# Short feed-forward: gate operands in steps between down-projection tiles, up-projection over 512 columns

## Chip, cores and metric

The kernel runs on one core of one Trainium2 chip. The metric is the device time of one execution in microseconds; a lower time is better.

## What is computed

A transformer layer is applied to two sequences with the same weights, a long one of 1024 tokens and a short one of 512, each with 16 learned tokens ahead. Everything is float32. Cut to what matters:

```python
n = rms_norm(h); qa, ka, va, qb, kb, vb = split(n @ w_in)
h = h + concat(gqa(qa, ka, va), diff_attention(qb, kb, vb)) @ w_out
n = rms_norm(h)
gate = n @ w_ff_gate                                   # 1024 -> 2816
gate = conv3_over_positions(gate) + conv_b             # depthwise, width 3
h = h + (gelu(gate) * (n @ w_ff_up)) @ w_ff_down       # 2816 -> 1024
y = rms_norm(h)[:, 16:]
```

## The kernel before

Activations lie transposed: features on the 128 partitions, tokens along the free dimension. The width of 1024 is 8 tiles (`KT`), the feed-forward width of 2816 is 22 tiles of 128 (`NFF`).

Float32 products are made of three matmuls. `split` (L111) turns an operand into a rounded part `hi` (a cast on ScalarE, ACT in the profile, L114) and the rest `lo` (a subtraction on VectorE or GpSimd, L115). `mm3` (L118) then issues hi x hi, hi x lo and lo x hi (L121 to L123). `dense` (L126) does that for the 8 tiles of the contraction: 24 matmuls into one PSUM tile.

`load_weight` (L171) fetches a 512 KB weight tile into a buffer `w_f` (2 of them) and splits it into `w_hi` and `w_lo` (3 of each in the short feed-forward). All loads and most stores are issued by SyncE (SP in the profile), whose queue is in order.

Order of the work: the short sequence's projection comes first, then its attention beside the long projection. Then the short sequence's output projection and feed-forward (`mixer_out`, `conv_glu`) run beside the long sequence's attention. Both are Python generators that yield their cost; `merge` (L1234) draws from them in the ratio of 1 to 0.4. That gives the program order. A scheduler that simulates a time line then sets each engine's order: among the instructions that it holds to be ready, the earlier in the program goes first. On the chip each engine keeps to the order so found. The rest, the long sequence's output projection and feed-forward, follows alone.

The short feed-forward, `conv_glu` with s = 1, N = 512, goes over the 22 tiles in groups of two (`grp`, f0 = 0, 2, ... 20):

1. Gate: per tile two chunks of 258 columns (256 and the neighbours that the convolution needs) through `dense`; the convolution on ScalarE and VectorE (L784 to L787) writes the tile `gate`, of which there is one buffer. One GELU over the group (L790).
2. Up: per tile the chunks of `centres = even_chunks(N, 510)`, two of 256 columns, through `dense`; VectorE multiplies the PSUM tile into `gate` (L802), and `split` makes `a_hi` (ScalarE) and `a_lo` (GpSimd) of it (L803).
3. Down: two weight tiles `wd`; 8 output tiles of 512 columns (`down`, L808), each of 2 x 3 matmuls, added to `h` by VectorE (L814).

PSUM has two banks for all of these ("mm").

The long feed-forward needs sums and differences of quarters of its first two gate weight tiles, split into hi and lo. `presplit` (L868) makes them ahead of time, in the short feed-forward's group f0 = 12 (`FPRE`): it loads the two raw weight tiles into the two `w_f` buffers, forms four sums of 512 columns on VectorE in a tile of the tag `gate` (L886, `minus` L881), and four times (`kept`, L874) splits a tile and stores both parts in DRAM (`wg`). Its order is `kept(0)`, the first raw tile as it is; two sums and `kept(1)`; two sums and `kept(2)`; `kept(3)`, half of the second raw tile. In the program all of it stands between the up- and the down-projection of that group, with two yields of cost 0. Since the two `wd` tiles hold two of the three `w_hi` buffers until the down-projection has ended, the splits share the third.

Of the kernel before, what the change touches and what calls it, by code (L numbers as in the profile page):

```python
# [15 lines left out]
ALU = mybir.AluOpType  # L16
# [36 lines left out]
def even_chunks(total, cap):  # L53
    cnt = -(-total // cap)
    w = -(-total // cnt)
    w += w % 2
    out, c = [], 0
    while c < total:
        out.append((c, min(w, total - c)))
        c += w  # L60
    return out
# [32 lines left out]
def pool(ctx, g, name, bufs, side):  # L94
    return ctx.enter_context(g.tc.tile_pool(name=name, bufs=bufs, side=side, reuse_waits="tile"))
# [15 lines left out]
def split(g, hi, lo, src, lo_engine=None):  # L111

    nc = g.nc
    return (nc.scalar.copy(hi, src).ins,  # L114
            (lo_engine or nc.vector).tensor_tensor(out=lo, in0=src, in1=hi.bitcast(F32), op=ALU.subtract).ins)  # L115
# [10 lines left out]
def dense(g, ps, w, xhi, xlo, c0, cw, order=range(KT)):  # L126

    for i, k in enumerate(order):
        last = mm3(g, ps, *block(w, k), xhi[k][:, c0:c0 + cw], xlo[k][:, c0:c0 + cw], i == 0, i == KT - 1)
    return last  # L130
# [17 lines left out]
def load_whole(wp, g, src, tag="w_f"):  # L148
    w = wp.tile([P, D], F32, name=tag, tag=tag, bufs=2)
    g.nc.sync.dma_start(out=w, in_=src)  # L150
    return w
# [19 lines left out]
def load_weight(g, wp, src, bufs=2, ahead=2, lo_engine=None):  # L171

    nc = g.nc
    w = wp.tile([P, D], F32, name="w_f", tag="w_f", bufs=ahead)
    nc.sync.dma_start(out=w, in_=src)
    hi = wp.tile([P, D], F32R, name="w_hi", tag="w_hi", bufs=bufs)
    lo = wp.tile([P, D], F32R, name="w_lo", tag="w_lo", bufs=bufs)
    passes = split(g, hi, lo, w, lo_engine)
    if g.splits is not None:
        g.splits.append(passes)  # L180
    return hi, lo
# [566 lines left out]
def conv_glu(ctx, g, s, st, side, wp, wb, gb):  # L748

    nc, tc = g.nc, g.tc  # L750
    N = SEQS[s]
# [5 lines left out]
    with tc.tile_pool(name=f"fn{s}", bufs=2, side=side, reuse_waits="tile") as np_:  # L757
        for c0, cw in token_chunks(s):
            for k in range(KT):
                t = np_.tile([P, cw], F32, name="t", tag="t")  # L760
                nc.vector.scalar_tensor_tensor(out=t, in0=h[:, k, c0:c0 + cw],
                                               scalar=g.gain[:, V_GFFN + k:V_GFFN + k + 1],
                                               in1=rstd[:, c0:c0 + cw], op0=ALU.mult, op1=ALU.mult)
# [3 lines left out]
    ap = pool(ctx, g, f"fa{s}", 2, side)  # L767
    centres = even_chunks(N, 510)
    for f0 in range(0, NFF, G):
# [5 lines left out]
        for f, c0, cw in ([(f, *c) for c in centres for f in grp] if f0 == 0 and s == 0 else  # L775
# [7 lines left out]
            a = gate[:, f - f0, c0:c0 + cw]  # L783
# [10 lines left out]
        for f in grp:  # L794
            wu = load_weight(g, wp, g.w_up[f], bufs=wb)
            ahi = ap.tile([P, N], F32R, name="a_hi", tag="a_hi", bufs=G + 1 - s)
            alo = ap.tile([P, N], F32R, name="a_lo", tag="a_lo", bufs=G + 1 - s)
            for c0, cw in centres:
                up = g.psum.tile(P, cw, "mm")
                dense(g, up, wu, xhi, xlo, c0 + 1, cw)  # L800
                a = gate[:, f - f0, c0:c0 + cw]
                nc.vector.tensor_tensor(out=a, in0=up, in1=a, op=ALU.mult)  # L802
                split(g, ahi[:, c0:c0 + cw], alo[:, c0:c0 + cw], a, nc.gpsimd)  # L803
                yield 24 * cw
            acts.append((ahi, alo))
        wd = [load_weight(g, wp, g.w_down[f], bufs=wb) for f in grp]

        def down(j, c0, cw):  # L808
            ps = g.psum.tile(P, cw, "mm")
            for i, ((ahi, alo), (dhi, dlo)) in enumerate(zip(acts, wd)):  # L810
                mm3(g, ps, dhi[:, j * P:(j + 1) * P], dlo[:, j * P:(j + 1) * P],
                    ahi[:, c0:c0 + cw], alo[:, c0:c0 + cw], i == 0, i == len(acts) - 1)
            hs = h[:, j, 1 + c0:1 + c0 + cw]
            nc.vector.tensor_tensor(out=hs, in0=ps, in1=hs, op=ALU.add)  # L814

        if f0 == FPRE:
            yield from presplit(g, wp, ap)
        if grp[-1] < NFF - 1:
            for j in range(KT):
                for c0, cw in even_chunks(N, 512):  # L820
                    down(j, c0, cw)
                    yield 3 * len(grp) * cw
            continue
        op = pool(ctx, g, f"fo{s}", 2, side)
        ob = 2 - s
        cw = 256
# [41 lines left out]
def presplit(g, wp, ap):  # L868

    nc = g.nc  # L870
    raw = [load_whole(wp, g, g.w_gate[i]) for i in range(2)]
    a11, a12, a21, a22 = (w[:, i * H:(i + 1) * H] for w in raw for i in range(2))

    def kept(i, src, w=D):  # L874
        hi = wp.tile([P, D], F32R, name="w_hi", tag="w_hi", bufs=3)[:, :w]
        lo = wp.tile([P, D], F32R, name="w_lo", tag="w_lo", bufs=3)[:, :w]
        split(g, hi, lo, src)
        for part, tl in enumerate((hi, lo)):
            nc.sync.dma_start(out=g.wg[i, part, :, :w], in_=tl.bitcast(F32))

    def minus(out, a, b):  # L881
        nc.vector.tensor_tensor(out=out, in0=a, in1=b, op=ALU.subtract)

    kept(0, raw[0])
    t = ap.tile([P, 2, H], F32, name="gate", tag="gate", bufs=1)
    nc.vector.tensor_tensor(out=t[:, 0], in0=a21, in1=a22, op=ALU.add)  # L886
    minus(t[:, 1], t[:, 0], a11)
    kept(1, t.rearrange("p x c -> p (x c)"))
    yield 0

    minus(t[:, 1], a12, t[:, 1])
    minus(t[:, 0], a11, a21)
    kept(2, t.rearrange("p x c -> p (x c)"))
    kept(3, a22, H)
    yield 0


def winograd(g, wp, up, x, raw, c0, cw, pre=None):
# [348 lines left out]
def drain(gen):  # L1247
    for _ in gen:
        pass
# [4 lines left out]
FPRE = 12  # L1254
# [16 lines left out]
def trunk_kernel(ctx, tc, g):  # L1271
# [82 lines left out]
    def sample():  # L1354
        yield from mixer_out(g, 1, st1, "left", wp, 3, "mm")
        yield from conv_glu(es1, g, 1, st1, "left", wp, 3, 1)
# [85 lines left out]
```

## Time and profile before

| | |
|---|---|
| median of 3 runs | 2126.57 us (2126.3 to 2130.99) |
| profiled execution | 2138.1 us, span 2136.3 us |
| mean granted TensorE clock | 0.982 |
| busy: TensorE matmul, weight load | 2051.1 us (96%), 1833.1 us (86%) |
| busy: VectorE, ScalarE, GpSimd | 1724.1 us (81%), 1156.8 us (54%), 582.7 us (27%) |
| HBM over the span | 138 GB/s |

PE is TensorE's matmuls, PEld its weight loads, DVE VectorE, ACT ScalarE, POOL GpSimd, and SPq the queue of SyncE. A row of the time line gives the start and the duration in us, the engine, the line, the operation, what it writes and reads, the shape and a count; in brackets the idle time of the engine ahead of it and what ended it. Matmuls are pipelined, so a matmul's duration overlaps the next one's. The profiled execution is 11.5 us longer than the median of the timed runs.

### The profile page before, as it was taken

To read this page: it belongs to the slowest core of one execution; us is meant where nothing else is said; L and a number is where in the kernel's file an instruction comes from. 1 tells how busy PE (TensorE), PEld (TensorE's weight loads), DVE (VectorE), ACT (ScalarE), POOL (GpSimd) and SP (SyncE) were. 2 spreads that over 40 slices of the span, in tenths; PEclk is the share of its full clock that TensorE was granted. 3 is DMA by queue.
4 is the path that set the end of the run, shared out by engine and by line. 5 is a ranking of instruction groups with operands and counts; after the bars stand their busy time and mean duration, and the time that the engine had idled before them with its cause. 6 is when DMAs were issued, how large, how long until landed. Compare 5 with 4: busy or idle time off the path is not lost.

```text
span 2136.3 us, 35264 instructions
## 1 busy us (share of the span) xinstructions
PE 2051.1 (96%) x12302; PEld 1833.1 (86%) x12302; DVE 1724.1 (81%) x3786; ACT 1156.8 (54%) x2253; POOL 582.7 (27%) x534
## 2 busy tenths in 40 slices
PE   6999999999999999999999999979999999999998
PEld 6988888997887999899989999978888777778877
DVE  6878889767879788888988885578878878869886
ACT  6635566544657556666666765345444444435454
POOL 4653233553112000000000000542444444330112
PEclk8999999999999999999999999998999999999999
DMA  7564335456621322223352224986232232247443
GB/s 252 178 198 133 118 110 170 153 182 226 206 84 55 105 75 70 70 85 114 103 188 77 93 88 145 300 256 229 101 109 89 97 115 84 94 166 258 119 126 126
DMA packets 164897, 296.30 MB, mean 139 GB/s; under 512 B 21456, under 2 KB 82672, under 8 KB 164208
## 3 DMA queue, kind: packets, MB, share of 16 engines
q1 hardware_dynamic: 162416, 287.76, 41.6%
q0 software_dynamic: 2304, 6.29, 0.8%
q8 instruction: 97, 1.59, 0.3%
q14 instruction: 80, 0.66, 0.1%
HBM read 211.13 MB, written 82.85 MB: 138 GB/s over the span
## 4 chain that ended last, share of the span: by engine, by line
PE 76%; DVE 12%; DMA 4%; ACT 3%; issue 3%; POOL 1%; SPq 1%; DVEq 0%; ACTq 0%; POOLq 0%
PE ps_mm L121 17%; PE ps_mm L123 17%; PE ps_mm L122 17%; PE ps_t L456 5%; PE ps_s L431 3%; PE ps_s L432 3%; PE ps_s L121 2%; PE ps_s L122 2%; PE ps_s L123 2%; PE ps_o L471 2%; PE ps_o L470 2%; DVE p L433 1%; DVE w_lo L115 1%; DMA m<-oT 1%; DVE acc L979 1%
## 5 line engine op out<-in xcount | busy, mean ns | idle before, releaser
L121 PE MATMUL ps_mm<-xhi,w_hi 128*128 128x258 f32 (+3 forms) x1264 | 383.4, 304 | 12.0 <-ACT xhi L114 3.7
L122 PE MATMUL ps_mm<-xlo,w_hi 128*128 128x258 f32 (+3 forms) x1264 | 379.0, 300 | 0.3 <-POOL xlo L115 0.3
L123 PE MATMUL ps_mm<-xhi,w_lo 128*128 128x258 f32 (+3 forms) x1264 | 377.2, 299 | 0.3 <-DVE w_lo L115 0.3
L433 DVE TENSOR_SCALAR_CACHE_REDUCE p<-ps_s 114x344 f32<-114x344 f32 (+4 forms) x562 | 257.6, 488 | 30.2 <-PE ps_s L432 19.1
L114 ACT CAST pt_hi<-ps_t 128x512 fp32r<-128x512 f32 (+6 forms) x360 | 169.3, 483 | 181.0 <-PE ps_t L456 155.2
L121 PEld LDWEIGHTS ps_mm<-xhi,w_hi 128*128 128x128 f32 x1264 | 240.0, 190 | 17.5 <-ACT xhi L114 5.4
L438 ACT ACTIVATE p<-p,nm 114x1040 f32<-114x1040 f32 (+5 forms) x212 | 214.8, 1013 | 72.8 <-DVE nm L436 71.8
L115 DVE TENSOR_TENSOR w_lo<-w_f,w_hi 128x1024 fp32r<-128x1024 f32 (+1 forms) x182 | 192.8, 1067 | 66.2 <-ACT w_hi L114 65.6
L122 PEld LDWEIGHTS ps_mm<-xlo,w_hi 128*128 128x128 f32 x1264 | 240.3, 190 | 1.9 <-POOL xlo L115 0.7
L123 PEld LDWEIGHTS ps_mm<-xhi,w_lo 128*128 128x128 f32 x1264 | 240.0, 190 | 1.2 <-DVE w_lo L115 0.5
L114 ACT CAST w_hi<-w_f 128x1024 fp32r<-128x1024 f32 (+1 forms) x199 | 167.6, 856 | 84.9 <-PE ps_mm L122 57.5
L115 DVE TENSOR_TENSOR pt_lo<-ps_t,pt_hi 128x512 fp32r<-128x512 f32 (+4 forms) x312 | 171.7, 561 | 43.7 <-ACT pt_hi L114 42.3
L115 POOL TENSOR_TENSOR a_lo<-gate,a_hi 128x256 fp32r<-128x256 f32 x44 | 43.3, 985 | 545.3 <-ACT a_hi L114 525.9
L431 PE MATMUL ps_s<-k,q 128*114 128x348 f32 (+4 forms) x552 | 183.6, 338 | 3.4 <-DVE p L433 3.2
L456 PE MATMUL ps_t<-ident,p 128*128 128x128 f32 (+7 forms) x1188 | 183.0, 270 | 1.0 <-DVE nm L436 0.5
L432 PE MATMUL ps_s<-k,q 128*114 128x348 f32 (+4 forms) x552 | 171.1, 315 | 0.0
L121 PE MATMUL ps_s<-xhi,w_hi 128*128 128x256 f32 (+4 forms) x480 | 148.7, 313 | 20.4 <-ACT xhi L234 8.2
L456 PEld LDWEIGHTS ps_t<-ident,p 128*128 128x128 f32 (+7 forms) x1188 | 140.4, 136 | 29.6 <-issue 6.8
L123 PE MATMUL ps_s<-xhi,w_lo 128*128 128x256 f32 (+4 forms) x480 | 147.4, 307 | 1.4 <-DMA w_lo<-wo 1.4
L122 PE MATMUL ps_s<-xlo,w_hi 128*128 128x256 f32 (+4 forms) x480 | 148.6, 310 | 0.0
L121 PE MATMUL ps_mm<-t_hi,w_hi 128*128 128x512 f32 (+2 forms) x368 | 144.6, 393 | 1.2 <-DVE v L934 1.2
L123 PE MATMUL ps_mm<-t_hi,w_lo 128*128 128x512 f32 (+2 forms) x368 | 144.4, 392 | 0.1
(275 smaller groups left out, 5309.4 us busy)
## 6 DMA issues: line engine op xcount, KB each, us to landing
w_f<-w_gate SPq DMA_DIRECT2D x46, 512.0 KB, 3.5
w_f<-w_up SPq DMA_DIRECT2D x44, 512.0 KB, 3.4
w_f<-w_in SPq DMA_DIRECT2D x36, 512.0 KB, 3.9
a_f<-act SPq DMA_DIRECT2D x62, 256.0 KB, 2.7
w_f<-w_down SPq DMA_DIRECT2D x22, 512.0 KB, 3.3
act<-a_t SPq DMA_DIRECT2D x44, 256.0 KB, 2.1
a<-w_down SPq DMA_DIRECT2D x40, 256.0 KB, 5.4
w_hi<-wo SPq DMA_DIRECT2D x36, 256.0 KB, 5.1
```

The costliest lines, as they stand in the source:

```text
L114: return (nc.scalar.copy(hi, src).ins, (lo_engine or nc.vector).tensor_tensor(out=lo, in0=src, in1=hi.bitcast(F32), op=ALU.subtract).ins)
L115: (lo_engine or nc.vector).tensor_tensor(out=lo, in0=src, in1=hi.bitcast(F32), op=ALU.subtract).ins)
L121: nc.tensor.matmul(ps, lhsT=whi, rhs=xhi, start=start, stop=False)
L122: nc.tensor.matmul(ps, lhsT=whi, rhs=xlo, start=False, stop=False)
L123: return nc.tensor.matmul(ps, lhsT=wlo, rhs=xhi, start=False, stop=stop).ins
L431: nc.tensor.matmul(ps, lhsT=q[0], rhs=k[:, c0:c0 + cw], start=True, stop=False)
L432: nc.tensor.matmul(ps, lhsT=q[1], rhs=k[:, c0:c0 + cw], start=False, stop=True)
L433: nc.vector.tensor_scalar(out=p[:, c0:c0 + cw], in0=ps, scalar1=HD ** -0.5, scalar2=-3.0e38, op0=ALU.mult, op1=ALU.max, accum_out=mx[:, i: ...
L438: g.last_exp = nc.scalar.activation(p, p, AF.Exp, bias=nm, accum_out=l).ins
L456: nc.tensor.transpose(tps[:, c:c + M], p[:, k0:k0 + kw], g.ident[:M, :M])
L470: nc.tensor.matmul(o, lhsT=v[:, i, :], rhs=hi, start=i == 0, stop=False)
L471: nc.tensor.matmul(o, lhsT=v[:, i, :], rhs=lo, start=False, stop=False)
```

## The change

1. The up-projection's chunks are `even_chunks(N, 512)`: one of 512 columns for the short sequence. Everything that runs by chunk (24 matmuls, the product L802, the split L803, the yield) runs once per tile over 512 columns.
2. `presplit` is no longer drawn as a whole ahead of the down-projection. One step of it is drawn after each of the group's 8 down-projection tiles (there are six steps, ended by five yields); what is left is drained behind them.
3. Its order of steps is: loads, two sums; `kept(1)`; two sums; `kept(2)`; `kept(0)`; `kept(3)`.
4. The four sums are made on GpSimd instead of VectorE.

```diff
-            for c0, cw in centres:
+            for c0, cw in even_chunks(N, 512):
                 up = g.psum.tile(P, cw, "mm")
                 dense(g, up, wu, xhi, xlo, c0 + 1, cw)
...
-        if f0 == FPRE:
-            yield from presplit(g, wp, ap)
         if grp[-1] < NFF - 1:
+            pre = presplit(g, wp, ap) if f0 == FPRE else iter(())
             for j in range(KT):
                 for c0, cw in even_chunks(N, 512):
                     down(j, c0, cw)
                     yield 3 * len(grp) * cw
+                next(pre, None)
+            drain(pre)
             continue
...
     def minus(out, a, b):
-        nc.vector.tensor_tensor(out=out, in0=a, in1=b, op=ALU.subtract)
-
-    kept(0, raw[0])
+        nc.gpsimd.tensor_tensor(out=out, in0=a, in1=b, op=ALU.subtract)
+
     t = ap.tile([P, 2, H], F32, name="gate", tag="gate", bufs=1)
-    nc.vector.tensor_tensor(out=t[:, 0], in0=a21, in1=a22, op=ALU.add)
+    nc.gpsimd.tensor_tensor(out=t[:, 0], in0=a21, in1=a22, op=ALU.add)
     minus(t[:, 1], t[:, 0], a11)
+    yield
     kept(1, t.rearrange("p x c -> p (x c)"))
-    yield 0
+    yield
 
     minus(t[:, 1], a12, t[:, 1])
     minus(t[:, 0], a11, a21)
+    yield
     kept(2, t.rearrange("p x c -> p (x c)"))
+    yield
+    kept(0, raw[0])
+    yield
     kept(3, a22, H)
-    yield 0
```

## The prediction

> **What bounds the kernel now.** I read the page's busy times first, then the busy time by stretches, then the instructions in order of time where a stretch falls short.
>
> ```profile
> span 2136.3 us, 35264 instructions
> ...
> PE 2051.1 (96%) x12302; PEld 1833.1 (86%) x12302; DVE 1724.1 (81%) x3786; ACT 1156.8 (54%) x2253; POOL 582.7 (27%) x534
> ```
>
> TensorE is busy nearly throughout. The changed code runs from about 690 to 1345 us, beside the attention of the long sequence. Columns of the stretches: length, then busy time of PE, PEld, DVE, ACT and POOL, then the granted TensorE clock, the DMA share and GB/s.
>
> ```profile
> 640.00:1060.00 420.00, 416.99 (x2819) 379.53 (x2820) 361.18 (x987) 264.00 (x465) 37.16 (x46) 1.00 0.27 84
> ...
> 1101.00:1123.00 22.00, 18.41 (x114) 16.90 (x113) 17.93 (x49) 13.73 (x26) 0.00 (x0) 0.84 0.52 176
> ```
>
> For 420 us TensorE has work at full clock: there only fewer or shorter matmuls save time, and DVE, ACT or POOL savings are worth nothing by themselves. The exception is 1101 to 1123 us, right behind the gate pair that the change moves (f0 = 12). There PE idles 3.6 us and the clock falls:
>
> ```profile
> 1090.00:1101.00 11.00, 10.53 (x57) 8.92 (x56) 11.00 (x25) 5.61 (x11) 0.00 (x0) 1.00 0.58 223
> ...
> 1112.80:1116.20 3.40, 0.31 (x4) 0.10 (x2) 3.05 (x8) 3.40 (x9) 0.00 (x0) 0.91 0.39 118
> 1116.20:1122.30 6.10, 6.10 (x24) 5.57 (x25) 4.20 (x12) 5.24 (x11) 0.00 (x0) 0.50 0.38 138
> ```
> ```profile
> 1112.82 0.28 PE L123 MATMUL ps_mm<-xhi,w_lo 128*128 128x258 f32 x1
> 1116.19 1.51 PE L545 MATMUL ps_o<-o_sq,ones_v 128*128 128x342 f32 x2 [3.09 <-ACT o_sq L543]
> ```
>
> I call this the hole. Its price: 3.1 us idle, 6.10 x (1 - 0.50) = 3.05 us lost at half clock, so 6.2 us. No other stretch of this stage offers as much.
>
> **Part 1: up-projection in one chunk of 512.** It replaces 22 x 2 x 24 = 1056 matmuls of 256 columns by 528 of 512. Matmuls overlap, so I price them by start to start: 14 steps between the first pair of rows (all rows between are of that kind), 9 between the second.
>
> ```profile
> 693.92 0.29 PE L121 MATMUL ps_mm<-xhi,w_hi 128*128 128x256 f32 x1
> ...
> 695.58 0.28 PE L123 MATMUL ps_mm<-xhi,w_lo 128*128 128x256 f32 x1
> ...
> 710.75 0.40 PE L121 MATMUL ps_mm<-a_hi,w_hi 128*128 128x512 f32 x1
> ...
> 712.85 0.40 PE L470 MATMUL ps_o<-pt_hi,v 128*128 128x512 f32 x1
> ```
>
> 1.66 / 14 = 118.6 ns and 2.10 / 9 = 233.3 ns. Two small ones cost 237.2, one large 233.3: 3.9 ns x 528 = 2.0 us saved, all on the path. The durations in the rows (0.28 against 0.40) would promise 0.16 x 528 = 84 us, but they include the overlap. The 528 weight loads that vanish ran beside matmuls already: nothing.
>
> The eviction is halved in number and grows in size, first the rows of now, then the nearest rows of 512 columns:
>
> ```profile
> L802 DVE TENSOR_TENSOR gate<-ps_mm,gate x44: 399/419/425, 690.2 to 1341.0; 128x256 f32<-128x256 f32 x44
> L114 ACT CAST a_hi<-gate x44: 388/406/420, 691.5 to 1341.8; 128x256 fp32r<-128x256 f32 x44
> L115 POOL TENSOR_TENSOR a_lo<-gate,a_hi x44: 728/766/1702, 691.9 to 1342.9; 128x256 fp32r<-128x256 f32 x44
> ```
> ```profile
> L114 ACT CAST w_hi<-a_f 128x512 fp32r<-128x512 f32 x62 | 38.5, 622 | 24.5 <-PE ps_mm L123 11.9 <-DMA a_f<-act 11.4 <-PE ps_mm L122 0.9
> ...
> L1024 DVE TENSOR_TENSOR act<-ps_mm,act 128x512 f32<-128x512 f32 x44 | 29.9, 679 | 0.8 <-ACT act L1016 0.8
> L1032 POOL TENSOR_TENSOR a_t<-act 128x512 f32<-128x512 f32 x22 | 28.8, 1310 | 27.3 <-DMA act<-act 22.4 <-DVE act L1024 4.9
> ```
>
> DVE: 44 x 0.419 - 22 x 0.679 = 3.5 us less; ACT: 44 x 0.406 - 22 x 0.622 = 4.2 us less; both beside a full TensorE, so zero. But the last chunk's way to the down-projection lengthens by 0.26 + 0.22 + 0.54 = 1.0 us, eleven times. What covers it now:
>
> ```profile
> 1079.48 0.28 PE L123 MATMUL ps_mm<-xhi,w_lo 128*128 128x256 f32 x1
> ...
> 1083.81 0.39 PE L122 MATMUL ps_mm<-a_lo,w_hi 128*128 128x512 f32 x1
> ```
> ```profile
> 1082.26 0.74 POOL L115 TENSOR_TENSOR a_lo<-gate,a_hi 128x256 fp32r<-128x256 f32 x1 [4.49 <-ACT a_hi L114]
> ```
>
> The last up matmul starts at 1079.48, its a_lo is ready at 1083.00 and first used at 1083.81; attention and the first operand's matmuls fill the time between. Of the 1.0 us, 0.8 is slack and 0.2 would be seen if the order stayed: eleven times 2 us; at most 11 us if no slack existed elsewhere; below nothing it cannot go by itself. The order of instructions is planned anew and TensorE has attention to put there, so I take 0. Sum of part 1: -2.0 us, bounds -2.0 and +9.
>
> **Part 2: the pair step by step, sums on GpSimd.** The work is the same: two weight loads, four sums of 512 columns, four splits, eight stores, in another place. Four DVE sums go (first and last shown; 0.68, 0.68, 0.68, 0.67 = 2.7 us):
>
> ```profile
> 1083.70 0.68 DVE L886 TENSOR_TENSOR gate<-w_f 128x512 f32<-128x512 f32 x1
> ...
> 1094.06 0.67 DVE L882 TENSOR_TENSOR gate<-w_f 128x512 f32<-128x512 f32 x1
> ...
> 1101.58 0.68 DVE L115 TENSOR_TENSOR w_lo<-w_f,w_hi 128x512 fp32r<-128x512 f32 x1
> ...
> 1104.09 1.21 DVE L115 TENSOR_TENSOR w_lo<-w_f,w_hi 128x1024 fp32r<-128x1024 f32 x1
> ```
>
> GpSimd gets 4 x 1.31 = 5.2 us (the a_t row); its queue is otherwise empty here, so nobody queues behind them. Whether the 2.7 us are worth anything depends on the chain that makes the hole:
>
> ```profile
> 1079.68 1.05 ACT L114 CAST w_hi<-w_f 128x1024 fp32r<-128x1024 f32 x1 [0.71 <-PE ps_mm L122]
> ...
> 1099.71 0.62 ACT L114 CAST w_hi<-w_f 128x512 fp32r<-128x512 f32 x1 [0.15 <-DMA wg<-w_hi]
> ...
> 1100.69 1.05 ACT L114 CAST w_hi<-w_f 128x1024 fp32r<-128x1024 f32 x1
> ...
> 1112.07 1.05 ACT L114 CAST w_hi<-w_f 128x1024 fp32r<-128x1024 f32 x1 [3.02 <-DMA w_f<-w_up]
> ```
> ```profile
> 1094.75 0.33 SPq L175 DMA_DIRECT2D w_f<-w_gate  x1
> ...
> 1102.65 0.42 SPq L175 DMA_DIRECT2D w_f<-w_gate  x1
> ...
> 1105.95 3.31 SPq L175 DMA_DIRECT2D w_f<-w_up  x2
> ```
> ```profile
> w_f<-w_gate SPq DMA_DIRECT2D x46, 512.0 KB, 3.5
> ```
>
> Read backwards: TensorE waits for o_sq on ACT; ACT had stood 3.02 us before a weight cast whose load (w_up[14]) had not landed, with the eviction of the gate product and o_sq queued behind it. That load was issued at 1105.95, right after its w_f buffer came free: the buffer's DVE split began at 1104.09 and took 1.21, though its cast was done at 1101.74. So DVE cost 2.35 us there. It also carried the pair's last split (1101.58), whose end at 1102.26 freed the other buffer for the load at 1102.65. A DVE that has done 2.7 us less by then can issue the load up to 2.35 us earlier, and the 3.02 us stand would shrink to 0.7.
>
> Against this stand two things. First, GpSimd sums slow DVE. This GpSimd instruction and the DVE one beside it, then the same DVE instruction without company:
>
> ```profile
> 700.62 0.73 POOL L115 TENSOR_TENSOR a_lo<-gate,a_hi 128x256 fp32r<-128x256 f32 x1 [3.37 <-ACT a_hi L114]
> ```
> ```profile
> 700.69 1.23 DVE L508 TENSOR_SCALAR p<-p,r 128x1040 f32<-128x1040 f32 x1
> ...
> 703.05 0.76 DVE L508 TENSOR_SCALAR p<-p,r 128x1040 f32<-128x1040 f32 x1
> ```
>
> 0.47 us are lost beside 0.73 us of GpSimd; four sums of that loss take back 1.9 of the 2.7, four of twice the length 3.8. The Trainium skill has a rule for it ("SBUF — State Buffer", Who interferes with whom): the shared port pair is an exclusive lock, and whoever comes second waits for the whole instruction. By that rule four sums could hold DVE for their full 5.2 us, more than it saves, and the hole would stay: the sum would be part 1 alone. The trace agrees that DVE waits (0.47 of the 0.66 us in which the two overlap).
>
> Second, the order. `kept(0)` moves from first to third of four splits, `kept(3)` stays last, and these two release the two w_f buffers that the next group's gate loads wait for. The splits now start every (1099.71 - 1079.68) / 3 = 6.7 us, since two of the three w_hi buffers are held by the down-projection and each split must be stored before the next. If `kept(0)` still runs first whenever its buffer is free and the sums aren't done, nothing is late. If it waits its turn, the first split starts when the two GpSimd sums end, at 1083.00 + 2 x 1.31 = 1085.6 plus waits, and the last one 6 us later than now. The eight stores and two loads also change places on SP; a store that waits for its split holds up the q loads behind it. Attention has q buffers in hand, so I put that at zero, at most one split's 6.7 us.
>
> I take half of the hole for part 2: 3.1 us gained, because the DVE relief is about half eaten by GpSimd. Bounds: 6.2 gained, 9.8 lost (rival C).
>
> **Sum.** -2.0 - 3.1 = -5.1 us. The profiled execution took 2138.1 us (span 2136.3), 11.5 over the median 2126.57, so a part of what it shows may not be in the timed runs; the hole depends on when a load lands, which is one more reason for half. On the median: 2126.6 - 5.1 = 2121.5.
>
> **Rivals.** A: the hole closes, -2.0 - 6.2 = 2118.4. For it: in 420 us of the same loop without the pair PE misses 3 us, so the pair alone makes the hole, and its own chain (2.35 us of DVE wait) is nearly as long as ACT's stand. It also closes with less than that if the half clock needs the whole idle: in the 420 us, with only short waits, the clock stays at 1.00, and 0.50 follows the one idle of 3.1 us. Then half of the idle removed takes all of the slow part with it: 1.5 + 3.05 + 2.0 = 6.6 us, 2120.0; of A's chance 0.07 is this. The Trainium skill states such a rule ("TensorE: Matmul & The Clock Gate", The two states you'll see): the array falls to half rate after an idle window of about 3.4 us. By it the sum is that 2120.0, and the trace agrees as far as its one idle goes.
>
> B: the hole stays, because DVE's relief is used up or the load is late for SP's sake: -2.0, 2124.6. For it: DVE is busy 11.00 of 11 us from 1090 to 1101, so what is taken off may be filled by attention at once, and the loads land when the DMA queues allow.
>
> C, slower: `kept(0)` and `kept(3)` hold the two w_f buffers longer. The next gate weights then come 6 to 7 us late, while FF has nothing else to give TensorE; a second idle of 6.7 with another 3.05 of half clock on top of a hole that stays: -2.0 + 9.8 = +7.8, 2134.4. It decides from 8.4 us of new waiting. For it: program order now puts `kept(0)` after the sums, and the load at 1102.65 follows its buffer's release at once. Against it: `kept(0)` needs no sum and finds the buffer free at 1079.68; the cast at 1100.69 came 2.4 us or so after its load could have landed (issue 1094.75, 3.5 us from issue to landing by the last row above), so the first weights have some slack.
>
> That the 512 chunk changes nothing is within the forecast: it is worth 2.0 us at most.
>
> **How the numbers follow.** Chances: forecast (part of the hole goes) 0.38, A 0.29, B 0.19, C 0.14. A measurement of this kernel tells 0.3%, 6.4 us, from no change: the line lies at 2120.2 and 2132.9. Faster: A, plus the part of the forecast that ends under 2120.2 (0.10) = 0.39. Slower: C less its mild half, plus waits of part 1, 0.13. Same: 0.48. The range reaches from A with 3 us to spare, 2115.5, to most of C, 2132; between them lie 0.82. The likeliest case's own range is 2119 to 2124.
>
> **What would show it.** Up matmuls of 512 columns with starts 0.233 us apart; four GpSimd sums around 1083 to 1095 us and no DVE sum of 512 columns there; the wait of the next group's weight cast for its w_up load under 1.5 us, and the granted clock near 1.00 in the 22 us behind the pair's down-projection. I am wrong if the stage behind it shows a longer wait of a cast for w_gate (C), if down matmuls wait for a_lo more than 2 us in all, or if the new order opens holes elsewhere in the stage, which no row of before can show.

## The result and the profile after

The change costs time: 2140.27 us median (2134.69 to 2145.5, five runs) against 2126.57 us. The ratio on record is 1.0052 (95% interval 1.0038 to 1.0067); these two medians alone give 1.0064. The forecast was 2121.5 us, in a range from 2115.5 to 2132.

The profiled execution of after was its shortest (2134.69), that of before (2138.1) longer than any of its timed runs; side by side these two would show a gain. So both kernels were profiled again, with the experiments: "before again" (span 2128.1) and "after again" (span 2139.1). Their difference, 11.0 us, is nearly that of their medians (2130.5 and 2141.06), and they are compared below.

First the two stretches of after that answer to the prediction's (columns as there). The stretch in which the hole stood is full and at full clock. But the gate pair now runs some 28 us earlier (its four GpSimd sums start from 1055.17 to 1064.48 us), so this stretch no longer lies right behind it; what became of the hole is read below, over 1050 to 1130 us.

```profile
640.00:1060.00 420.00, 415.77 (x2490) 362.23 (x2488) 349.92 (x919) 256.78 (x432) 34.30 (x34) 1.00 0.26 83
...
1101.00:1123.00 22.00, 22.00 (x126) 19.47 (x125) 19.25 (x50) 16.69 (x29) 1.40 (x1) 1.00 0.34 107
```

The up-projection's rows in the time line of after start 0.23 us apart, as priced:

```profile
691.60 0.39 PE L121 MATMUL ps_mm<-xhi,w_hi 128*128 128x512 f32 x1
691.83 0.39 PE L122 MATMUL ps_mm<-xlo,w_hi 128*128 128x512 f32 x1
692.06 0.39 PE L123 MATMUL ps_mm<-xhi,w_lo 128*128 128x512 f32 x1
```

The loss lies elsewhere. The next two fences show, for before again and after again, when two kinds of instruction ran: L802, VectorE's product of the up-projection, and L433, VectorE's eviction of the attention scores. After the count come the shortest, median and longest duration in ns, then the first and the last start in us (L433's first belongs to the short sequence).

```profile
L802 DVE TENSOR_TENSOR gate<-ps_mm,gate x44: 398/419/425, 686.9 to 1335.6; 128x256 f32<-128x256 f32 x44
L433 DVE TENSOR_SCALAR_CACHE_REDUCE p<-ps_s x562: 401/508/522, 162.5 to 1257.5; 114x344 f32<-114x344 f32 x72, 128x344 f32<-128x344 f32 x64, 128x264 f32<-128x264 f32 x21, 102x264 f32<-102x264 f32 x16
```
```profile
L802 DVE TENSOR_TENSOR gate<-ps_mm,gate x22: 672/690/692, 689.4 to 1301.5; 128x512 f32<-128x512 f32 x22
L433 DVE TENSOR_SCALAR_CACHE_REDUCE p<-ps_s x562: 401/509/523, 163.1 to 1296.1; 114x344 f32<-114x344 f32 x72, 128x344 f32<-128x344 f32 x64, 128x264 f32<-128x264 f32 x21, 102x264 f32<-102x264 f32 x16
```

Before, the last scores were evicted at 1257.5 us, and the up-projection went on until 1335.6. After, the up-projection ends at 1301.5 and the last scores come only at 1296.1. The short feed-forward has run ahead of the long attention, so that little is left beside the attention's end. What that costs is in the busy times by stretches, before again and then after again:

```profile
1250.00:1300.00 50.00, 49.75 (x356) 46.74 (x355) 34.57 (x69) 28.67 (x55) 4.06 (x4) 1.00 0.40 134
1300.00:1350.00 50.00, 49.78 (x361) 49.30 (x360) 23.60 (x61) 23.20 (x46) 16.15 (x20) 1.00 0.71 210
1350.00:1400.00 50.00, 48.23 (x307) 45.98 (x306) 29.86 (x52) 18.79 (x44) 26.89 (x37) 1.00 0.95 303
```
```profile
1250.00:1300.00 50.00, 50.00 (x317) 45.99 (x316) 41.84 (x112) 31.68 (x58) 1.29 (x1) 1.00 0.25 76
1300.00:1350.00 50.00, 46.63 (x307) 42.43 (x306) 27.31 (x69) 23.82 (x57) 6.65 (x8) 0.97 0.44 124
1350.00:1400.00 50.00, 43.57 (x255) 39.33 (x254) 30.27 (x51) 20.38 (x48) 30.57 (x44) 1.00 0.97 324
```

From 1300 to 1400 us PE was busy 98.0 us, now 90.2, and 1.4 us more go at the lower clock (0.03 of 46.63). The waits of PE in after again from 1294 to 1400 us (total, times, longest) are those of a chain with little beside it: the attention's last normalisations (o_sq, o_rs) and the start of the long output projection (operands xhi, weights wo from DRAM).

```profile
PE ps_s L121 <- ACT xhi L114: 2.5, 2, 1.9
PE ps_s L121 <- DMA w_hi<-wo: 2.1, 4, 1.5
PE ps_s L123 <- DMA w_lo<-wo: 1.5, 3, 0.9
PE ps_o L545 <- ACT o_sq L543: 1.3, 2, 1.1
PE ps_o L466 <- DVE o_rs L106: 0.9, 1, 0.9
```

**A measure for all runs.** "Lost" is worked out from the starts of the matmul rows: each step from one start to the next, less the median step between the same two kinds where PE stands full (before again, 690 to 1000 us; 0.233 us for the 512-column matmuls). It holds idle time and slow clock alike. How finely the kinds are told apart moves the differences between kernels in the first "lost" column by up to 4 us, in the two behind it by about 1. "Cover" is the feed-forward work left behind the attention's last score matmul: its matmul rows times their step, without the last group's down-projection (96 rows of 256 columns, 11.3 us), which lies behind the last score in every kernel but two_evict and before_mm3, where 12 of its rows do. One profiled execution stands for each kernel: up512_only's was its slowest (2.5 us over its median), up512_late's its fastest (3.1 us under). All in us:

| kernel | ratio (95% interval) | cover | lost: first up product to last score | last score to last down-projection | from there to first long gate product | span |
|---|---|---|---|---|---|---|
| before again | 0.9996 (0.9984 to 1.0008) | 45.4 | 27.0 | 4.0 | 19.9 | 2128.1 |
| steps_only | 1.0015 (1.0002 to 1.0027) | 46.2 | 26.7 | 4.3 | 19.8 | 2128.2 |
| steps_dve | 0.9997 (0.9985 to 1.0009) | 45.4 | 24.7 | 4.5 | 19.0 | 2126.9 |
| mid_steps | 1.0015 (1.0004 to 1.0027) | 39.7 | 25.4 | 4.6 | 21.7 | 2133.1 |
| up512_mid | 0.9987 (0.9976 to 0.9998) | 36.7 | 22.0 | 4.0 | 23.0 | 2123.0 |
| up512_late | 1.0001 (0.999 to 1.0013) | 32.0 | 22.0 | 4.3 | 25.2 | 2125.3 |
| one_evict | 1.0007 (0.9996 to 1.0019) | 31.3 | 25.2 | 4.3 | 21.2 | 2130.9 |
| up512_early | 1.0036 (1.0022 to 1.005) | 12.1 | 25.2 | 8.1 | 24.2 | 2137.4 |
| up512_only | 1.0053 (1.0037 to 1.0069) | 7.7 | 24.3 | 13.5 | 26.0 | 2143.9 |
| after again | 1.0045 (1.003 to 1.006) | 5.6 | 27.5 | 12.4 | 21.1 | 2139.1 |
| two_evict | 1.0132 (1.0112 to 1.0152) | 0 | 26.4 | 21.6 | 28.5 | 2152.5 |
| before_mm3 | 1.0166 (1.0148 to 1.0185) | 0 | 42.4 | 19.9 | 30.4 | 2168.6 |
| up512_paced | 1.007 (1.0056 to 1.0085) | 40.6 | 38.1 | 5.0 | 23.6 | 2146.7 |
| after_paced | 1.008 (1.0066 to 1.0094) | 40.9 | 38.0 | 7.1 | 25.4 | 2150.5 |
| after_fine | 1.0132 (1.0115 to 1.0149) | 41.3 | 49.2 | 4.7 | 26.0 | 2158.8 |
| up512_fine | 1.0151 (1.0131 to 1.0171) | 41.1 | 53.2 | 4.6 | 25.5 | 2161.8 |

The measure closes to about 1 us: over the whole span, the 2.0 us of saved steps taken off, it gives after again +9.9 against before again (spans +11.0) and two_evict +24.3 (spans +24.4).

### The profile page after: what moved, and what is told of

Its sections match the earlier page's. It is cut to its first block, busy times and chain, and to the rows that moved or that the text cites. A ratio compares the mean times of both kernels' runs of the same rounds, so it can differ in the third digit from the quotient of the medians.

```text
span 2132.9 us, 34150 instructions
## 1 busy us (share of the span) xinstructions
PE 2047.8 (96%) x11774; PEld 1798.5 (84%) x11774; DVE 1724.4 (81%) x3760; ACT 1153.0 (54%) x2231; POOL 585.2 (27%) x516
## 3 DMA queue, kind: packets, MB, share of 16 engines
q1 hardware_dynamic: 162416, 287.76, 41.3%
## 5 line engine op out<-in xcount | busy, mean ns | idle before, releaser
L121 PE MATMUL ps_mm<-xhi,w_hi 128*128 128x258 f32 (+4 forms) x1088 | 353.4, 325 | 11.3 <-ACT xhi L114 4.2
L122 PE MATMUL ps_mm<-xlo,w_hi 128*128 128x258 f32 (+4 forms) x1088 | 349.2, 321 | 0.4 <-POOL xlo L115 0.3
L123 PE MATMUL ps_mm<-xhi,w_lo 128*128 128x258 f32 (+4 forms) x1088 | 347.3, 320 | 0.3 <-DVE w_lo L115 0.3
L433 DVE TENSOR_SCALAR_CACHE_REDUCE p<-ps_s 114x344 f32<-114x344 f32 (+4 forms) x562 | 259.2, 489 | 32.2 <-PE ps_s L432 20.2
L121 PEld LDWEIGHTS ps_mm<-xhi,w_hi 128*128 128x128 f32 x1088 | 206.8, 190 | 22.2 <-ACT xhi L114 5.9
L122 PEld LDWEIGHTS ps_mm<-xlo,w_hi 128*128 128x128 f32 x1088 | 206.9, 190 | 8.3 <-POOL xlo L115 0.8
L123 PEld LDWEIGHTS ps_mm<-xhi,w_lo 128*128 128x128 f32 x1088 | 206.7, 190 | 7.4 <-DVE w_lo L115 0.7
L115 POOL TENSOR_TENSOR a_lo<-gate,a_hi 128x512 fp32r<-128x512 f32 x22 | 33.5, 1524 | 511.2 <-ACT a_hi L114 511.2
L122 PE MATMUL ps_mm<-t_lo,w_hi 128*128 128x512 f32 (+2 forms) x368 | 143.1, 389 | 0.0
```

What stands on the lines that cost most here:

```text
L121: nc.tensor.matmul(ps, lhsT=whi, rhs=xhi, start=start, stop=False)
L122: nc.tensor.matmul(ps, lhsT=whi, rhs=xlo, start=False, stop=False)
L123: return nc.tensor.matmul(ps, lhsT=wlo, rhs=xhi, start=False, stop=stop).ins
L433: nc.vector.tensor_scalar(out=p[:, c0:c0 + cw], in0=ps, scalar1=HD ** -0.5, scalar2=-3.0e38, op0=ALU.mult, op1=ALU.max, accum_out=mx[:, i: ...
```

## The experiments

Theories, by the letters that the expectations use: H, the handover at the attention's end, which has lost its cover; L, the 512-column product by itself (longer hold of its PSUM bank, longer way to a_lo); P, the pair; G, VectorE slowed by the GpSimd sums; R, raw weight buffers released late.

**Which part.** up512_only has part 1 alone, steps_only parts 2 to 4; the other two are the kernels themselves.

```diff
 up512_only, against before:
-            for c0, cw in centres:
+            for c0, cw in even_chunks(N, 512):
```

> Part 1 alone: up-projection in one chunk of 512 columns, presplit as in the kernel before. Theory H (handover): with one PSUM bank holding 512 up columns the short feed-forward gets further ahead of the long attention; it runs out of up products some 40 us earlier and the stretch from the end of the ups to the end of the long output projection, which has less to fill TensorE with, loses what is lost: this kernel is slower than before by 8 to 14 us and its last up product lies before 1310 us. Theory P (pair): the loss comes from the gate pair's new place, so this kernel gains the 2 us of the larger matmuls: 0 to 4 us faster than before, last up product near 1340 us.

> Part 2 alone: the gate pair in steps with GpSimd sums, up-projection in two chunks of 256. Theory H: within 5 us of before (the hole of 6 us exchanged for smaller waits). Theory P: slower than before by 8 to 14 us, with waits of TensorE for late gate weights of f0 = 14 of 8 us or more.

> The kernel before once more, as a control with a second profile: its span was 2136 us in the profiled execution and some 2125 us in the timed ones. Theories H and P: ratio 1.000 within 0.003. If the hole of 6 us behind the pair belongs to single executions alone, it is shorter here; if it belongs to the order of instructions, TensorE again stands 3 us at that place.

> The changed kernel once more, as a control with a second profile: 1.005 times before again (8 to 14 us slower) if that is a property of the kernel and not of the chip it ran on. Theory H: the stretch from the last up product to the end of the long output projection misses 15 us or more of TensorE time than in the kernel before; theory P: the stretch behind the pair does.

Part 1 alone carries the whole loss: 1.0053 against 1.0052 and 1.0045 with the pair, so P falls. Part 2 alone comes to 1.0015, within the 0.3% called no change. The table puts part 1's loss behind the last score: 13.5 against 4.0 us, then 26.0 against 19.9; ahead of it part 1 loses no more than before (24.3 against 27.0, less apart than the measure can tell). In after again it is 12.4 against 4.0, then 21.1 against 19.9. H had put 15 us or more behind the last up product of after again; counted from there to the first long gate product it is some 12, so the place was right and the size was not.

**Holding the feed-forward back by groups, taking the cover away with 256 columns, and the sums on VectorE.** In the paced kernels the gate products of group n (from the third) may stand on PE only behind the attention block behind which they stood before:

```diff
 after_paced, up512_paced, against after and up512_only:
+PACE = [22, 26, 28, 31, 33, 36, 38, 40, 42, 45, 47]
...
+            hold = [g.tails[PACE[f0 // 2] - 1]] if f0 // 2 >= 2 else []
...
-                dense(g, gp, wg[f], xhi, xlo, c0, cw + 2)
+                with behind(g, *hold):
+                    dense(g, gp, wg[f], xhi, xlo, c0, cw + 2)
 before_mm3, against before:
-    g.psum = Psum(tc, "psa", mm=2, s=3, t=2, o=1)
+    g.psum = Psum(tc, "psa", mm=3, s=2, t=2, o=1)
 steps_dve, against steps_only:
-        nc.gpsimd.tensor_tensor(out=out, in0=a, in1=b, op=ALU.subtract)
+        nc.vector.tensor_tensor(out=out, in0=a, in1=b, op=ALU.subtract)
...
-    nc.gpsimd.tensor_tensor(out=t[:, 0], in0=a21, in1=a22, op=ALU.add)
+    nc.vector.tensor_tensor(out=t[:, 0], in0=a21, in1=a22, op=ALU.add)
```

> The changed kernel with the pace of before: from the third group of the short feed-forward on, its gate products stand on TensorE behind that attention block behind which they stood in the kernel before (block 28, 31, 33, 36, 38, 40, 42, 45, 47 of 48). The matmuls of 512 columns and the pair's steps stay. Theory H (the loss is the handover: the feed-forward has run out when the attention ends): the loss goes, 2126 to 2133 us, the last up product again behind 1325 us and the time from the last up product's PSUM read to the end of the long output projection misses as little as in the kernel before. Rival L (the loss is the longer way from an up product of 512 to the down-projection, or the larger matmul itself): still 8 to 14 us slower than before.

> Part 1 alone with the pace of before (as after_paced, but the gate pair as in the kernel before). Theory H: 2 us faster than before for the larger matmuls, within 2122 to 2130 us, and 10 us or more faster than part 1 alone without the pace. Rival L: 2140 us, as part 1 alone.

> The kernel before with its chunks of 256, but three PSUM banks for the feed-forward's products and two for the attention's scores instead of two and three. No chunk is changed; the feed-forward runs ahead as in the changed kernel (groups start behind blocks 23, 25, 28, 30, 32, 35, 37, 38, 40, 41, 42 of 48, and no up product is left when the last scores are issued). Theory H: slower than before by 8 to 20 us, lost between 1290 and 1450 us. Rival L: not slower by more than 4 us, or lost before 1290 us (fewer score banks).

> Part 2 alone with the four sums on VectorE as in the kernel before (steps and their order as changed). If GpSimd's sums cost VectorE what they save (theory G), this is the same as part 2 alone, 1.0015 times before, within 2 us. If the later release of the two raw weight buffers is what keeps the hole (theory R), also the same, but TensorE's waits behind the pair come with casts that wait for w_gate or w_up, and they are as long as in part 2 alone (5 to 6 us of TensorE time from 1100 to 1125 us). If the sums on GpSimd are what keeps the hole, it is 3 us faster than part 2 alone.

The hold gives the cover back (40.6 us) and with it the end: 5.0 us lost there instead of 13.5. But it loses 38.1 instead of 24.3 us ahead of the last score, and the sum is slower: H's times for both paced kernels (2133 and 2130 us at most) missed by 17 us or more. So it shows the place, not a remedy. before_mm3 has chunks of 256 columns, as before, but one PSUM bank more for them and one less for the scores. Its feed-forward ends first, the cover is 0, and the last two columns of lost time rise by 26.4 us without any 512-column up-projection. It is slower than H's 8 to 20 us (1.0166, some 35 us); that it also loses 42.4 ahead of the last score, with a bank less for the scores, keeps it from being a clean test.

**Finer holds, and doses.** The fine holds put every gate and up product behind the very score matmul behind which it stood before:

```diff
 up512_fine, after_fine, against up512_only and after:
-                dense(g, up, wu, xhi, xlo, c0 + 1, cw)
+                with behind(g, *mark(UPS, f)):
+                    dense(g, up, wu, xhi, xlo, c0 + 1, cw)
 (the gate products in the same way, with the table GATES)
 up512_late, up512_early, against before:
-            for c0, cw in centres:
+            for c0, cw in even_chunks(N, 512) if f0 >= 12 else centres:   # early: f0 < 10
```

> The 512-column up-projection alone, but each product of the gate and each product of the up-projection may stand on TensorE only behind the attention score matmul behind which it stood in the kernel before. This is a finer hold than that by groups: it gives back the old interleaving of feed-forward and attention (26 first-product rows of 512 columns, that is 52 of 256, left when the last score is issued; 64 in the kernel before, 8 without the hold). Theory H (the loss is the end of the attention, which has lost the feed-forward that covered it): the time lost on TensorE between the last score and the last down-projection falls from the 13.5 us of the 512-column kernel without holds to about 4 to 6, the long output projection starts without its extra, and the time comes to 0.998 to 1.002 of the kernel before, at least 6 us under the 512-column kernel without holds. Theory L (512 columns cost by themselves: longer way from product to a_lo, two banks held longer): the time stays at 1.004 to 1.007. If the holds themselves cost, as the holds by groups did, the loss from the first up-product to the last score rises from 27 towards 38 us and the ratio is 1.005 or more with a low loss behind the last score: then H stays shown for the place and not for the sum.

> The whole change, with the same fine holds behind the attention's scores. Theory H: 0.999 to 1.004 of the kernel before (the pair's part adds its 0.0015), at least 5 us under the changed kernel without holds. Theory L: as the changed kernel, 1.004 to 1.007. If the holds cost by themselves: 1.006 or more, with the loss between the first up-product and the last score above 35 us.

> 512 columns in the last five groups of the short feed-forward alone (f0 from 12), 256 in the first six; the rest as in the kernel before. In the order of instructions 16 first-product rows of the up-projection are left at the last score and 40 of the down-projection at the last value product: about half of the cover is kept. Theory H: less than half of the loss, 1.000 to 1.003, and a loss on TensorE between last score and last down-projection of 4 to 9 us. Theory L (a cost of each 512-column product by itself): five elevenths of the loss, 1.0025, spread over the groups behind 1080 us.

> The mirror: 512 columns in the first five groups alone (f0 under 10), 256 in the last six. 32 first-product rows of 256 columns are left at the last score, but only 8 of the down-projection at the last value product, as with 512 columns everywhere. Theory H: the loss lies again behind the last score (8 us or more until the last down-projection), although the five groups nearest to it are those of the kernel before; 1.002 to 1.005. Theory L: five elevenths of the loss, 1.0025, spread over the groups before 1030 us, and behind the last score as in the kernel before (4 us).

The fine holds lose even more ahead of the last score (53.2 us), so the forecast of H for the sum missed; its proviso, that holds may cost, held. The waits of PE from 690 us to the last score, in up512_fine and then in before again, show the form of that cost:

```profile
PE ps_s L431 <- DVE p L433: 10.0, 13, 2.2
PE ps_o L470 <- DVE o_a L489: 2.3, 2, 1.1
```
```profile
PE ps_o L545 <- ACT o_sq L543: 2.7, 1, 2.7
PE ps_mm L121 <- DVE h L814: 0.4, 1, 0.4
```

With the old places but lumps of 24 x 0.233 = 5.6 us instead of two of 2.8, PE comes to the scores while VectorE is still evicting. That wait is 10.0 us of the 26 that are lost in addition; that the lumps are its reason is argued, not shown. What the holds do show is that 512-column matmuls with the cover kept (41 us) lose 4.6 us up to the last down-projection, not 13.5.

The doses went by H in the place. Five groups of 512 columns late keep 32 us of cover and lose 4.3 us up to the last down-projection, as before; their ratio is 1.0001. Five groups early leave 12.1 us of cover and lose 8.1 us there, although the groups nearest to that end are those of before; L had put 4 us there. Each has ten tiles, so a cost of each product by itself would be the same in both. The ratios alone decide less: up512_late's holds a gain of 5.0 us ahead of the last score, where the hole has closed, against 5.3 us more in the last column; and up512_early's interval includes L's 1.0025.

The last column does not follow the cover as the one ahead of it does: up512_late has 25.2 us with 32 us of cover, after again 21.1 with 5.6. Some 4 to 6 us more than before stand in this column in up512_only, up512_late, up512_early and the held kernels alike, and their cause stays open.

**What lets the feed-forward run ahead: the bank and the way, or the matmul.** one_evict keeps one PSUM tile, one product and one split of 512 columns and fills the tile with matmuls of 256; two_evict has matmuls of 512 and evicts in halves.

```diff
 one_evict, against up512_only:
+            up = g.psum.tile(P, N, "mm")
-            for c0, cw in even_chunks(N, 512):
-                up = g.psum.tile(P, cw, "mm")
-                dense(g, up, wu, xhi, xlo, c0 + 1, cw)
+            for c0, cw in centres:
+                dense(g, up[:, c0:c0 + cw], wu, xhi, xlo, c0 + 1, cw)
 (then one product and one split over N)
 two_evict, against up512_only:
+            up = g.psum.tile(P, N, "mm")
+            dense(g, up, wu, xhi, xlo, 1, N)
-            for c0, cw in even_chunks(N, 512):
+            for c0, cw in centres:
                 (product and split of each half)
 up512_mid, against before; mid_steps, against steps_dve:
+            for c0, cw in even_chunks(N, 512) if f0 in (12, 14) else centres:
```

> One PSUM tile of 512 columns, one product and one split of 512 columns as in the changed kernel, but filled by 2 x 24 matmuls of 256 columns; the pair as before. In the order of instructions 32 first-product rows of 256 columns are left at the last score and 52 of the down-projection at the last value product (64 and 64 in the kernel before, 11 rows of 512 and 8 in the 512-column kernel). Theory H (loss by the attention's end without cover, whatever moves it): the time goes with the cover, some 30 us of feed-forward work left at the last score, 1.000 to 1.002. Theory L (the longer hold of the bank and the longer way to a_lo cost by themselves): 1.004 or more, since both are as in the 512-column kernel.

> 24 matmuls of 512 columns, but product and split in two halves of 256 columns, so that the last half's way to a_lo is the short one; the pair as before. In the order of instructions no up-projection row is left at the last score and 8 of the down-projection. Theory H: the loss is that of the 512-column kernel or more, 1.004 to 1.009, behind the last score. Theory L: the way is short again, so less than half of the loss stays, 1.000 to 1.003.

> 512 columns in the two groups f0 = 12 and 14 alone, the rest as in the kernel before. 39 first-product rows of 256 columns are left at the last score, and 64 of the down-projection at the last value product as before. Theory H: cover nearly kept (35 to 40 us), no loss behind the last score; the matmul steps of two groups save 0.4 us and the stretch of idle and half clock behind the pair may close (3 to 5 us), since the pair has moved: 0.997 to 1.000. Theory L: two elevenths of the loss, 1.001.

> 512 columns in the groups f0 = 12 and 14 alone, and the pair in steps between the down-projection tiles, with its sums on VectorE. 48 first-product rows are left at the last score, 64 of the down-projection at the last value product. Theory H: 0.996 to 1.000, the best of these kernels if the idle stretch behind the pair closes. Theory L: 1.001.

This separates them. The last starts of the up product and of the score eviction, and the stretch behind them, in one_evict and then in two_evict:

```profile
L802 DVE TENSOR_TENSOR gate<-ps_mm,gate x22: 672/684/693, 694.2 to 1315.4; 128x512 f32<-128x512 f32 x22
L433 DVE TENSOR_SCALAR_CACHE_REDUCE p<-ps_s x562: 400/508/523, 161.9 to 1270.7; 114x344 f32<-114x344 f32 x72, 128x344 f32<-128x344 f32 x64, 128x264 f32<-128x264 f32 x21, 102x264 f32<-102x264 f32 x16
...
1300.00:1350.00 50.00, 49.39 (x359) 47.93 (x359) 26.08 (x67) 24.62 (x51) 14.17 (x16) 1.00 0.51 145
```
```profile
L802 DVE TENSOR_TENSOR gate<-ps_mm,gate x44: 412/418/426, 688.6 to 1279.0; 128x256 f32<-128x256 f32 x44
L433 DVE TENSOR_SCALAR_CACHE_REDUCE p<-ps_s x562: 401/507/523, 162.6 to 1309.7; 114x344 f32<-114x344 f32 x72, 128x344 f32<-128x344 f32 x64, 128x264 f32<-128x264 f32 x21, 102x264 f32<-102x264 f32 x16
...
1300.00:1350.00 50.00, 40.44 (x238) 35.04 (x237) 28.95 (x81) 27.55 (x62) 0.87 (x2) 0.93 0.45 130
```

With the long hold and the long way of the 512-column tile, but small matmuls, the scores still end 45 us ahead of the up-projection and the time is that of before (1.0007). With the short way but large matmuls they end 31 us behind it, PE is idle 9.6 of 50 us in the stretch shown, and the ratio is 1.0132, more than twice the change's loss and more than H had said (0.9% at most). So L falls as far as bank and way go. one_evict and up512_only differ in the size of the matmul alone, with the same tiles, evictions and yields. A matmul of 512 columns moves the order that the planner makes, and with that order the cover goes. Why the planner places the larger matmul so no run shows.

up512_mid, where only the two groups about the pair take 512 columns, is the only kernel with its whole interval under 1: 0.9987, 2.8 us, within the 0.3% called no change here. Its saved steps are 0.4 us; what it gains is the hole. mid_steps, forecast to be the best, missed: 1.0015. Its feed-forward and cover are nearly the same, but part 2 is in it, and PE is idle 3.3 us of the 80 about the pair where up512_mid's is idle 0.5.

## Why the prediction was wrong, point by point

**Part 1, the steps: right.** 0.233 us apart, 2.0 us less work; evictions took 0.69 us for 512 columns as priced (0.679), beside other work.

**Part 1, the order: this step failed.** The prediction said: "The order of instructions is planned anew and TensorE has attention to put there, so I take 0." It priced the new order only as the last chunk's way to the down-projection. That TensorE always has attention to put in held until 1256 us only because the feed-forward lagged behind. By the table the term, taken at 0, is +9.6 us behind the last score in after again (12.4 + 21.1 against 4.0 + 19.9), 8.4 of it up to the last down-projection, and +15.6 in up512_only, whose profiled execution was its slowest. The 8.4 go with the cover; of the rest that stays open. The bound of +9 stood for another mechanism, the longer way to a_lo; one_evict, which has that way and the bank's longer hold, comes to 1.0007 (1.0019 at most), though its order moved too. The sign named last ("the new order opens holes elsewhere in the stage, which no row of before can show") came true at the stage's end and behind it, but rows of before could have shown the danger: in before again the last score at 1257.5 and the last up product at 1335.6 mean that 45 us of feed-forward work covered the attention's end.

**Part 2, half of the hole: not gained.** The stretch about the pair, 1050 to 1130 us, in before again, steps_only, steps_dve, after again and up512_mid:

```profile
1050.00:1130.00 80.00, 76.27 (x525) 71.87 (x525) 71.42 (x196) 53.63 (x101) 3.63 (x4) 0.98 0.46 155
```
```profile
1050.00:1130.00 80.00, 75.50 (x521) 70.21 (x520) 73.50 (x204) 55.00 (x105) 8.77 (x8) 1.00 0.46 155
```
```profile
1050.00:1130.00 80.00, 78.44 (x538) 73.49 (x536) 73.99 (x204) 56.98 (x105) 3.63 (x4) 0.98 0.44 151
```
```profile
1050.00:1130.00 80.00, 74.68 (x457) 66.43 (x456) 72.14 (x193) 53.93 (x98) 9.78 (x7) 1.00 0.46 155
```
```profile
1050.00:1130.00 80.00, 79.50 (x483) 71.30 (x482) 72.84 (x195) 57.94 (x102) 4.54 (x3) 1.00 0.44 149
```

Idle plus slow clock: before again 3.73 + 0.02 x 76.27 = 5.3 us; steps_only 4.5; steps_dve 1.56 + 1.57 = 3.1; after again 5.3; up512_mid 0.5. So the one hole became several short waits of the same sum; after again's are, for 1050 to 1130 us:

```profile
PE ps_mm L121 <- ACT w_hi L114: 1.9, 1, 1.9
PE ps_o L468 <- DVE pt_lo L115: 1.4, 1, 1.4
PE ps_s L431 <- DVE p L433: 1.2, 1, 1.2
```

The cause that the prediction gave for the hole is gone, as it said: the weight cast for w_up waited 2.78 us for its load in before again and 0.45 in after again.

```profile
1108.39 1.05 ACT L114 CAST w_hi<-w_f 128x1024 fp32r<-128x1024 f32 x1 [2.78 <-DMA w_f<-w_up]
```
```profile
1086.12 1.05 ACT L114 CAST w_hi<-w_f 128x1024 fp32r<-128x1024 f32 x1 [1.86 <-DMA w_f<-w_gate]
...
1092.89 1.06 ACT L114 CAST w_hi<-w_f 128x1024 fp32r<-128x1024 f32 x1 [0.45 <-DMA w_f<-w_up]
```

What is late next is what failed: PE waits for weight casts and VectorE splits beside the pair itself. Its longest wait there, 1.87 us, points to a term that the prediction put at zero, the new places of the pair's stores on SP. In after again the next group's two w_gate loads are issued among them, and the first cast starts 7.1 us after its load's issue, against the 3.5 us from issue to landing that the prediction took:

```profile
1078.59 0.32 SPq L880 DMA_DIRECT2D wg<-w_lo  x1
1079.00 1.06 SPq L175 DMA_DIRECT2D w_f<-w_gate  x1
1080.15 1.02 SPq L880 DMA_DIRECT2D wg<-w_lo  x1
```
```profile
1087.21 0.39 PE L121 MATMUL ps_mm<-xhi,w_hi 128*128 128x258 f32 x1 [1.87 <-ACT w_hi L114]
```

The cast of 1086.12 is the one that this matmul waits for; that the stores slowed its load is argued from their places. The hole of before had such a load too: in the prediction's own rows the w_up load issued at 1105.95 is waited for until 1112.07, 6.1 us, so its lateness was not VectorE's 2.35 us alone. And VectorE's sums alone did not make the hole: up512_mid leaves the pair, its place in the program and its VectorE sums as before, and loses 0.5 us about it. Rival C's sign did not come: the w_gate cast waits 1.86 us in after again and 2.17 in before again. Whether the sums' engine is to blame stays open: steps_dve and steps_only differ by 0.0018 with intervals that overlap, and mid_steps, with VectorE sums, is as slow as steps_only.

## What to carry over

Where two streams share the bound engine, look for which of them ends first and what is left to cover the end of the other: here 45 us of feed-forward work stood behind the attention's last score, and with 8 to 0 us of it left 10 to 26 us more of TensorE time are lost behind that score, more than the 5 us that the change was to save. An edit that changes the size of an instruction changes the planned order too; compare the last instruction of each stream, before and after, ahead of pricing the instructions. The new order may help or harm by more than the saved steps: 512 columns in two groups of eleven closed the hole (0.9987), in all of them they took the cover away (1.0053).

## What the runs showed of the hardware

The length of a wait did not tell what the clock would do. In after again 5.3 us of idle, in waits of at most 1.9, ran at 1.00. In before again one idle of 2.74 us was followed by 6 us at 0.72 (first row). But in steps_dve waits of only 1.06 and 0.38 us, before the matmuls at 1099.96 and 1101.06, were followed by 3 us at 0.66 (second row).

```profile
1112.50:1118.50 6.00, 5.99 (x33) 5.73 (x34) 5.11 (x16) 4.93 (x11) 0.00 (x0) 0.72 0.43 151
```
```profile
1101.00:1104.00 3.00, 2.94 (x15) 2.86 (x16) 2.82 (x15) 3.00 (x6) 0.00 (x0) 0.66 0.92 291
```

The Trainium skill ("TensorE: Matmul & The Clock Gate", The two states you'll see) puts the fall behind an idle window of about 3.4 us; here 2.74 us of idle were enough, in steps_dve far less, and the measurement decides. So the prediction's variant of rival A, that the half clock needs the whole idle, was not safe.

For the GpSimd sums, this is a row of GpSimd in after and then two of VectorE, each over one column:

```profile
1055.17 1.44 POOL L886 TENSOR_TENSOR gate<-w_f 128x512 f32<-128x512 f32 x1
```
```profile
1055.45 0.15 DVE L442 RECIPROCAL r<-l 114x1 f32<-114x1 f32 x1
1055.63 1.00 DVE L531 SCALAR_TENSOR_TENSOR c<-r,neglam,l 114x1 f32<-114x1 f32 x1
```
```profile
L531 DVE SCALAR_TENSOR_TENSOR c<-r,neglam,l x56: 202/218/1049, 306.2 to 1261.0; 114x1 f32<-114x1 f32 x36, 102x1 f32<-102x1 f32 x12, 104x1 f32<-104x1 f32 x8
```

L531 takes 0.218 us as a rule (the last row, before again) and here 1.00, until 1056.63, when the sum ends (1056.61). This agrees with the rule of the Trainium skill ("SBUF — State Buffer", Who interferes with whom) that the port pair that the two engines share is locked for a whole instruction; the reciprocal beside the same sum was not held up (0.15 us). The prediction's 0.47 of 0.66 us may be another case of it, though less than the whole overlap was lost there.
